# Two-layer trunk step on one core: parked latents spread over the head boundaries, two latent weights split early and parked, the last neighbourhood head and the first latent heads in another order

## The chip, the cores and the metric

The kernel runs on one core of one Trainium2 chip. The metric is device microseconds of one execution; the time before is the median of three runs, 1476.01 us (1475.26 to 1476.55). Engines are called PE (matmul), PEld (its weight loads), DVE (vector), ACT (scalar), POOL (GpSimd) and SP (which issues nearly all DMAs).

## The reference, cut to what matters

One denoising step of a two-layer backbone on 512 latent tokens and 128 prompt tokens. Layer 0 has eight latent-attention (MLA) heads and eight neighbourhood-attention heads over the same normed input; the change touches only this layer.

```python
def even_project(h, w_in, q_norm, w_uq, kv_norm, w_ukv):
    p = h @ w_in
    cq, ckv, krope, nq, nk, nv = jnp.split(p, [i0, i1, i2, i2 + na_w, i2 + 2 * na_w], axis=-1)
    q = (rms_norm(cq, q_norm) @ w_uq).reshape(b, L, MLA_HEADS, MLA_QK_DIM)
    ckv = rms_norm(ckv, kv_norm)
...
    a_mla = attend_blocked(q, jnp.concatenate([k_lat, k_ctx], axis=1),
                           jnp.concatenate([v_lat, v_ctx], axis=1), MLA_SCALE)
    a_na = neighbourhood_attention(nq, nk, nv, c_nk, c_nv, rpb)
    return jnp.concatenate([a_mla.reshape(b, L, -1), a_na.reshape(b, L, -1)], axis=-1) @ w_out
```

Neighbourhood attention lets a token see a window of 8 by 16 grid neighbours, with a bias, and 128 cached prompt tokens, in one softmax. The latent heads get their keys and values by multiplying the compressed latents `ckv` with `w_ukv`, and their queries by multiplying `cq` with `w_uq`.

## The kernel before, in words

All products are done in high and low parts: a float32 operand is copied to a reduced-precision "high" part by ACT and the rest, "low", is formed by a subtraction on DVE (for some on POOL). A product is then three matmuls, or two where one side needs no low part. A name that ends in h or l is such a part. `unit` (line 168) loads a weight into a raw buffer and splits it this way; there are three raw buffers (`rawp`, line 72) and three for split weights (`wp`).

The queue of each engine is put in order by a scheduler at build time, which may draw an instruction ahead of others that are written before it. `tc.issue_after` (through the helper `after`, line 177) bounds that: of what is issued inside it, those instructions that run on the given instruction's own engine get their places behind it, those of other engines are not held. The order of PE's work is written by hand in strings of piece names, which `sequence` (line 121) runs, each piece's matmuls behind the last matmul ahead of it. A piece issues its matmuls and the ACT, DVE and POOL work that takes their result out of PSUM.

The neighbourhood heads go one after another (line 945). Of head h, `s0` and `s1` are the score matmuls (tiles `ns`) and their softmax (`np`); `t0` to `t2` transpose the probabilities of the head before (`nt`) and split them (`nts`), `v0` to `v2` multiply them with the values (`no`), after which `half_sum` (line 411) copies half of the result (`nhs`, ACT) and adds (DVE into `oN`). `q` pieces are projections of later heads' queries and keys (`nq`, `nk`), `m` pieces are parts of a modulation product (`mod`, fed by loads `mraw`), `pt` and `pv` are transposes and values for the prompt tokens of a head pair (`npp0t`, `npp0o` and so on).

During this the latents `ckv`, `cq` and the rotary key `kr` leave the SBUF: `park` (line 845) splits each 128x640 piece (ACT `pt...h`, DVE `pt...l`) and SP stores the halves in DRAM (`pk...`). The temporaries are three buffers of one ring (`tmp`, line 103), so a fourth temporary waits until an earlier store has landed. `PARK_AT` (line 861) gives the head ahead of which each is parked; it is issued behind `PE.last`, the last matmul at that time, which holds none of it, since nothing of it runs on PE; the scheduler has put nearly all of it ahead of head 0's scores.

The last head (h = 7, the last string of `NA_ORDER`) has the first latent pieces among its own: `k0` and `k1` (`mk`) are keys of the first head pair, `u0` and `u1` (`mq`) queries of head 0. `k_set` (line 889) splits the keys. `latents`, `unpark` and `k_rope` load the parked data back. `wmv` is the value weight of all latent heads, `wm0` to `wm3` (line 838) are the key and query weights of a pair of heads, and `mv_of` makes one of six value blocks (`b0` to `b5` or `mv`): two in the row of pieces after the last head (line 1001), four after it (line 1072). The table `tq` (640 KB, line 1008) is needed for the queries of latent head 1 and later.

The latent heads (line 1080) run by `MLA_ORDER`: `s0` to `s3` are scores (`ms`) of 128 queries each, with a maximum on DVE (`mn`) and an exponential on ACT (`mp`), two score banks being there; `q0`, `q1` and `k0`, `k1` are queries of the next head (`mq`, then `mqt` on DVE, `mqh` on ACT, `mql` on POOL) and keys of the next pair; `t`, `v` and `l` are transposes (`mt`, `mts`) and value products (`mo`) of the head before.

Of the kernel before, what the change touches and what calls it, by code (L numbers as in the profile page):

```python
# [18 lines left out]
P = 128  # L19
# [32 lines left out]
def body(ctx, tc, xT, vecs, crow, wm0, wm0g1, wm0g, wm1, wA, wNV, wNA, wMK, wMV, wOA, wGQ, wGK, wGV, wOC,  # L52
# [109 lines left out]

    def load(src, n, name):
        raw = rawp.tile([P, 1024], F32, tag="raw", name=name)
        nc.sync.dma_start(raw[:, :n], src)
        return raw[:, :n]

    def unit(src, n, name, lo="v", pool=None, bufs=3):

        raw = load(src, n, name + "r")  # L170
# [240 lines left out]
    def half_sum(dsts, ps, n, pool, name):  # L411

        t = pool.tile([64, 512], F32, tag="hs", bufs=1, name=name)
        S.activation(t[:, :n], ps[64:128, :n], AF.Copy)
        for dst, a, b in dsts:
            V.tensor_tensor(dst, ps[0:64, a:b], t[:, a:b], ALU.add)

# [285 lines left out]
    nqk, wnas = {}, {}  # L703
# [77 lines left out]
    def na_scores(h, bm, pts):  # L781
# [5 lines left out]
        def piece(jj):  # L787
# [6 lines left out]
            for j in (2 * jj, 2 * jj + 1):  # L794
# [3 lines left out]
                S.activation(pt, pt, AF.Exp, bias=mm[:, j:j + 1], scale=-1.0, accum_out=ll[:, j:j + 1])  # L798
# [4 lines left out]
    def na_values(h, pts, o):  # L803
# [16 lines left out]
        def av(n):  # L820
            def run():
# [7 lines left out]
                if n == 2:  # L829
                    half_sum(((o[rr, 64:NS], 0, 448), (o[rr, 0:64], 448, NS)), box["o"], NS, ab, f"nhs{h}")  # L830
# [5 lines left out]
    wmk = {}  # L836
# [19 lines left out]

    def cached_latents():
# [4 lines left out]
               3: lambda: park("cq0", cq[0], T), 4: lambda: park("cq1", cq[1], T), 5: lambda: park("kr", kr, 768)}  # L862

    def latents():
# [12 lines left out]
    def unpark(name):  # L877
        out = [ring.tile([P, T], F32R, tag="h" + c, name=f"{name}{c}") for c in "hl"]
        for t, d in zip(out, parked[name]):
            nc.sync.dma_start(f(t), d)  # L880
# [8 lines left out]
    def k_set(r, rows, parts, src, p=0):  # L889

        jobs = []
        for c in parts:
            c0, c1 = KPART[c]
            o = c0 - KPART[parts[0]][0]
            h, l = [(prompt if c == 2 else main_[:, c0:c1])[rows] for main_, prompt in k_tiles(r, p)]
            jobs.append((h, l, src[rows, o:o + c1 - c0]))
# [11 lines left out]
    def k_pieces(p, bk):  # L908

        out = {}  # L910
        for c, n in ((0, 512), (1, 256)):
            parts = ((0,), (1, 2))[c]

            def done(ps, parts=parts):
                for r in range(2):
                    k_set(r, slice(64 * r, 64 * r + 64), parts, ps, p)
# [26 lines left out]
    NA_ORDER += ["s0 t0 t1 pt s1 m0 v0 t2 sp m1 v1 pv m2 v2", "s0 t0 t1 k0 s1 v0 t2 sp k1 v1 u0 v2 u1"]  # L943
    M_AT = 1, 3, 5, 6
    for h in range(8):
# [5 lines left out]
        if h in PARK_AT:  # L951
            after(PE.last, PARK_AT[h])
# [17 lines left out]
        if h == 7:  # L970
            cqs = after(PE.last, lambda: [unpark(f"cq{u}") for u in range(2)])
# [7 lines left out]
        if h == 6:  # L979
            mla_w(0)  # L980
            lat = latents()
# [4 lines left out]
            wmv = unit(wMV, 1024, "wmv")  # L986
        if h == 7:
            for r in range(2):
                k_rope(r, (slice(64, 128), slice(0, 64))[r])
# [1151 lines left out]
```

## Time and profile before

| | |
|---|---|
| median of three runs | 1476.01 us |
| the profiled execution's own time | 1476.62 us |
| its span in the trace | 1474.5 us |
| TensorE clock granted over it | 0.996 |
| ACT, DVE, POOL busy | 783.3, 1231.4, 175.0 us |

The span is counted from the first instruction; about 2.1 us of the execution's time lie outside of it. The stretch of the neighbourhood heads is 94 to 213 us on the trace's clock, the latent heads follow up to about 320 us. In a row of the timeline the columns are start, duration, engine, line, operation, output and inputs, form, count, and in brackets the idle time of the engine ahead of it with what ended it. PE's rows overlap: one starts before the modelled end of the row ahead, so the step from start to start is the cost of a matmul.

### The profile page before, as it was taken

Reading aid. Unit: us, or ns where it says so; the run is one execution under the profiler, and the core shown is the slowest. Engines: PE = TensorE matmul, PEld = TensorE weight load, DVE = VectorE, ACT = ScalarE, POOL = GpSimd, SP = SyncE. Lnnn points to the kernel's source line nnn. Section 1 sums busy time; section 2 is a strip of 40 time slices with the busy share of each in tenths; the row PEclk is TensorE's granted clock in tenths of the full one; section 3 lists DMA queues with packets and bytes.
Section 4 is the critical chain, followed back from the end, with each engine's and each line's share of the span. In section 5 each row is a group of like instructions: output and inputs, shape, how many; then the busy total and the mean of one; then the engine's idle time right before and its main releaser. Section 6 shows DMA issues by size and latency. Waiting matters only on the chain.

```text
span 1474.5 us, 25877 instructions
## 1 busy us (share of the span) xinstructions
PE 1440.1 (98%) x9764; PEld 1390.1 (94%) x9764; DVE 1231.4 (84%) x2350; ACT 783.3 (53%) x1530; POOL 175.0 (12%) x270
## 2 busy tenths in 40 slices
PE   5999999999999999999999999999999999999997
PEld 4988888889999999999999999989999999999997
DVE  5877668877898989965997888888899898989976
ACT  5446667763755555541122666672656555555443
POOL 0037545430000000000000122220000000000000
PEclk9999999999999999999999999999999999999999
DMA  9655471026165555569764310115245555548572
GB/s 369 211 185 194 135 243 46 15 73 200 47 202 173 168 168 170 173 223 326 241 220 155 101 34 30 43 37 194 84 169 178 184 174 185 174 147 294 185 270 72
DMA packets 84884, 239.22 MB, mean 162 GB/s; under 512 B 9496, under 2 KB 15800, under 8 KB 84376
## 3 DMA queue, kind: packets, MB, share of 16 engines
q1 hardware_dynamic: 82400, 233.16, 47.2%
q10 hardware_dynamic: 1944, 3.48, 0.7%
q8 instruction: 76, 1.25, 0.4%
q0 software_dynamic: 416, 0.93, 0.2%
q14 instruction: 48, 0.39, 0.1%
HBM read 197.21 MB, written 40.33 MB: 161 GB/s over the span
## 4 chain that ended last, share of the span: by engine, by line
PE 83%; DVE 7%; ACT 4%; DMA 3%; issue 2%; DVEq 0%; ACTq 0%; POOL 0%; SPq 0%
PE fg L64 19%; PE fd L64 9%; PE fgo L64 5%; PE fo L64 5%; PE fu L64 4%; PE gq L64 3%; PE fdo L64 2%; PE gs L64 2%; PE go L64 2%; PE nk L64 1%; PE fuo L64 1%; DMA mraw<-in_wm 1%; PE gt L68 1%; PE mod L64 1%; ACT mp L1036 1%
## 5 line engine op out<-in xcount | busy, mean ns | idle before, releaser
L1708 DVE SCALAR_TENSOR_TENSOR junk<-wm,cb 128x1024 bf16<-128x1024 f32 x88 | 107.4, 1220 | 4.6 <-DMA wm<-in_wm 3.7
L64 PE MATMUL gq<-h10h,wgq 128*128 128x320 f32 x256 | 65.8, 316 | 0.0
L267 POOL TENSOR_SCALAR h10h<-h10t,gs,mods 128x320 fp32r<-128x320 f32 x4 | 3.9, 990 | 430.1 <-DVE h10t L261 427.7
L1448 ACT ACTIVATE wY<-s 128x1024 fp32r<-128x1024 f32 x38 | 40.3, 1061 | 27.4 <-PE fg L64 22.5
L1448 ACT ACTIVATE wZ<-s 128x1024 fp32r<-128x1024 f32 x38 | 40.2, 1057 | 21.1 <-PE fd L64 16.0
L1976 POOL TENSOR_TENSOR xr<-xw,fn1rs 128x320 f32<-128x320 f32 x2 | 1.7, 861 | 412.8 <-ACT fn1rs L235 412.8
L1449 DVE TENSOR_TENSOR wZ<-s,wZ 128x1024 fp32r<-128x1024 f32 x38 | 46.4, 1222 | 2.5
L1449 DVE TENSOR_TENSOR wY<-s,wY 128x1024 fp32r<-128x1024 f32 x38 | 46.3, 1220 | 0.3
L64 PEld LDWEIGHTS gq<-h10h,wgq 128*128 128x128 f32 x256 | 44.9, 189 | 0.6
L1557 DVE TENSOR_TENSOR sg<-up,sg 128x640 f32<-128x640 f32 x38 | 31.3, 823 | 15.9 <-ACT sg L1556 14.9
L1556 ACT ACTIVATE sg<-fg 128x320 f32<-128x320 f32 x38 | 16.7, 438 | 48.4 <-PE fg L64 48.4
L1578 ACT ACTIVATE p<-fd 128x320 f32<-128x320 f32 x38 | 16.6, 437 | 46.3 <-PE fd L64 46.3
L64 PE MATMUL gq<-h10l,wgq 128*128 128x320 f32 x128 | 39.4, 308 | 0.0
L1913 ACT ACTIVATE gp<-gs,gb,rq 128x640 f32<-128x640 f32 (+1 forms) x40 | 31.8, 796 | 13.2 <-DVE gb L1912 11.8
L64 PE MATMUL fg<-h01E,wW 128*128 128x320 f32 x228 | 36.6, 309 | 0.7 <-DVE g L1588 0.7
L64 PE MATMUL fg<-h01N,wZ 128*128 128x320 f32 x228 | 36.6, 309 | 0.5 <-ACT p L1576 0.5
L64 PE MATMUL fg<-h11N,wZ 128*128 128x320 f32 x228 | 36.7, 309 | 0.0
L64 PE MATMUL fg<-h01q,wX 128*128 128x320 f32 x228 | 36.7, 309 | 0.0
L64 PE MATMUL fu<-h11q,wX 128*128 128x320 f32 x228 | 36.6, 309 | 0.0
L64 PE MATMUL fd<-h01q,wZ 128*128 128x320 f32 x228 | 36.6, 309 | 0.0
L64 PE MATMUL fd<-h11q,wZ 128*128 128x320 f32 x228 | 36.6, 309 | 0.0
L64 PE MATMUL fg<-h11q,wX 128*128 128x320 f32 x228 | 36.5, 309 | 0.0
(3416 smaller groups left out, 5296.0 us busy)
## 6 DMA issues: line engine op xcount, KB each, us to landing
wm<-in_wm SPq DMA_DIRECT2D x48, 512.0 KB, 4.3
mraw<-in_wm SPq DMA_DIRECT2D x8, 1024.0 KB, 13.1
mraw<-in_wm SPq DMA_DIRECT2D x14, 512.0 KB, 4.3
wmv<-in_wm0g SPq DMA_DIRECT2D x8, 512.0 KB, 4.1
wm<-in_wm0g SPq DMA_DIRECT2D x8, 512.0 KB, 4.7
ruo<-in_wFO SPq DMA_DIRECT2D x8, 512.0 KB, 4.3
rgo<-in_wFO SPq DMA_DIRECT2D x8, 512.0 KB, 5.5
x<-in_xT SPq DMA_DIRECT2D x8, 320.0 KB, 5.6
```

What stands on the lines that cost most here:

```text
L64: cls.last = nc.tensor.matmul(*a, **k)
L68: cls.last = nc.tensor.transpose(*a, **k)
L267: G.tensor_scalar(h[:, c0:c1], t, self.gsl[:, k, 0:1], self.ml[:, self.sh + k, 0:1], ALU.mult, ALU.add)
L1036: exps[h, j] = S.activation(halves(pt), pss[:, :, :HT], AF.Exp, bias=nm, accum_out=ll[:, j:j + 1])
L1448: S.activation(h, src, AF.Copy)
L1449: V.tensor_tensor(w_, src, f(h), ALU.subtract)
L1556: last = S.activation(sg[:, 0:HT], g[:, :HT], AF.Silu, scale=-1.0)
L1557: V.tensor_tensor(sg, up, sg, ALU.mult)
L1578: S.activation(p5, b5[:, :HT], AF.Copy)
L1708: V.scalar_tensor_tensor(junk, raw, 1.0, cb[:, c, :], ALU.mult, ALU.mult, accum_out=mods[l][:, j0 + i, c:c + 1])
L1913: gexp[h, j] = S.activation(dst, src, AF.Exp, bias=nb, scale=rq[:, j:j + 1], accum_out=ll[:, j:j + 1])
L1976: G.tensor_tensor(x[k][:, c0:c1], root[1][k], nrm.rs[:, c0:c1], ALU.mult)
```

## The change

It has five parts.

1. **Parking.** `PARK_AT[h]` is issued behind the last exponential of head h-1, an ACT instruction, instead of behind `PE.last`. So its ACT copies, and what follows from them on DVE and SP, are spread over the boundaries ahead of heads 1 to 5.
2. **Third and fourth latent weights.** `park_weights` loads `wm2` ahead of head 3 and `wm3` ahead of head 5, splits them in two pieces of 128x384 (ACT `ptwm`, the same ring of three temporaries; DVE in place) and stores them. When they are needed they come as four loads, and ACT and POOL split nothing there. `wm1` is still split, but behind `half_sum` of head 7.
3. **Last neighbourhood head.** `s1` goes directly behind `s0`; the split of `wmv` goes behind the last exponential of head 7; the parked latents are loaded behind `wm0`'s load, `cq` behind `wmv`'s, the rotary keys behind `cq`'s. `b0` and `b1` go ahead of `pt`. `k_set` does the high parts of all four tiles ahead of the low parts.
4. **First latent heads.** Heads 0 and 1 have an order of their own.
5. **A value block.** Block 5 is made between `s2` and `s3` of latent head 0.

```diff
     def mla_w(p):
         if p not in wmk:
-            wmk[p] = unit(wMK[p], 768, f"wm{p}", lo="g")
+            if f"wm{p}" in parked:
+                t = wp.tile([P, 2, 1024], F32R, tag="w", bufs=3, name=f"wm{p}")
+                for c, d in enumerate(parked[f"wm{p}"]):
+                    nc.sync.dma_start(f(t[:, c, :768]), d)
+                wmk[p] = [t[:, c, :768] for c in range(2)]
+                return wmk[p]
+            wmk[p] = after(done_with[7] if p == 1 else None, lambda: unit(wMK[p], 768, f"wm{p}", lo="g"))
         return wmk[p]
...
+    def park_weights(p):
+
+        raw = load(wMK[p], 768, f"wmp{p}r")
+        parked[f"wm{p}"] = [drc.tile([P, 768], F32, name=f"pkwm{p}{c}") for c in "hl"]
+        dh, dl = parked[f"wm{p}"]
+        for a, b in ((0, 384), (384, 768)):
+            h = tmp(f"ptwm{p}{a}")[:, :b - a]
+            S.activation(h.bitcast(F32R), raw[:, a:b], AF.Copy)
+            V.tensor_tensor(raw[:, a:b].bitcast(F32R), raw[:, a:b], h, ALU.subtract)
+            nc.sync.dma_start(dh[:, a:b], h)
+        nc.sync.dma_start(dl, raw)
...
-               3: lambda: park("cq0", cq[0], T), 4: lambda: park("cq1", cq[1], T), 5: lambda: park("kr", kr, 768)}
+               3: lambda: (park("cq0", cq[0], T), park_weights(2)), 4: lambda: park("cq1", cq[1], T),
+               5: lambda: (park("kr", kr, 768), park_weights(3))}
...
-    NA_ORDER += ["s0 t0 t1 pt s1 m0 v0 t2 sp m1 v1 pv m2 v2", "s0 t0 t1 k0 s1 v0 t2 sp k1 v1 u0 v2 u1"]
+    NA_ORDER += ["s0 t0 t1 pt s1 m0 v0 t2 sp m1 v1 pv m2 v2", "s0 s1 t0 t1 k0 v0 t2 sp k1 v1 u0 v2 u1"]
...
         if h in PARK_AT:
-            after(PE.last, PARK_AT[h])
+            after(nexps[h - 1, 3], PARK_AT[h])
...
-            cqs = after(PE.last, lambda: [unpark(f"cq{u}") for u in range(2)])
+            cqs = after(fetched["wmvr"], lambda: [unpark(f"cq{u}") for u in range(2)])
...
-            lat = latents()
+            lat = latents(fetched["wm0r"])
...
-            wmv = unit(wMV, 1024, "wmv")
+            wmvr = load(wMV, 1024, "wmvr")
         if h == 7:
-            for r in range(2):
-                k_rope(r, (slice(64, 128), slice(0, 64))[r])
+            wmv = after(nexps[7, 3], lambda: unit(None, 1024, "wmv", raw=wmvr))
+            with tc.issue_after(fetched["cq1"].ins):
+                for r in range(2):
+                    k_rope(r, (slice(64, 128), slice(0, 64))[r])
...
-    BESIDE = ()
+    BESIDE = (5,)
...
+    FIRST_ORDER = "s0 q0 s1 q1 s2 b5 s3", "k0 s0 q0 s1 t0 t1 q1 s2 v0 k1 l0 t2 s3 v1 t3 l1 v2 l2 t4"
...
-        sequence(MLA_ORDER[r], {**pieces, **late, **{k: v for k, v in tail.items() if k not in ("v3", "v4", "l3", "l4")}})
+        sequence(FIRST_ORDER[h] if h < 2 else MLA_ORDER[r], {**pieces, **late, **{k: v for k, v in tail.items() if k not in ("v3", "v4", "l3", "l4")}})
```

What stands in the queues at three places, before and now. A row gives the line, the operation, output and inputs, and the size.

First, ACT ahead of head 0, before: `ptckv10h`, `ptcq00h` and `ptcq10h` are parked latents, `nqh` and `nk` the high parts of head 0's and 1's queries and keys, `wnk` the next weight.

```order
L852 ACTIVATE ptckv10h<-ckvr_753 128x640
L724 ACTIVATE nqh_1021<-nq_1032 64x256
L724 ACTIVATE nqh_1022<-nq_1032 64x256
L724 ACTIVATE nqh_1021<-nq_1065 64x192
L173 ACTIVATE wnk_1191<-wnk1r 128x1024
L724 ACTIVATE nqh_1022<-nq_1065 64x192
L852 ACTIVATE ptcq00h<-cqr_594 128x640
L724 ACTIVATE nqh_1021<-nq_1065 64x128
L753 ACTIVATE nk_1030<-nk_1102 64x256
L852 ACTIVATE ptcq10h<-cqr_599 128x640
L724 ACTIVATE nqh_1022<-nq_1065 64x128
L753 ACTIVATE nk_1031<-nk_1102 64x256
```

The same place now:

```order
L727 ACTIVATE nqh_1021<-nq_1032 64x256
L727 ACTIVATE nqh_1022<-nq_1032 64x256
L727 ACTIVATE nqh_1021<-nq_1065 64x192
L175 ACTIVATE wnk_1191<-wnk1r 128x1024
L727 ACTIVATE nqh_1022<-nq_1065 64x192
L727 ACTIVATE nqh_1021<-nq_1065 64x128
L756 ACTIVATE nk_1030<-nk_1102 64x256
L727 ACTIVATE nqh_1022<-nq_1065 64x128
L756 ACTIVATE nk_1031<-nk_1102 64x256
```

The three parked pieces are gone from here, and their low parts from DVE likewise.

Second, ACT between the end of head 2 and head 3, before: `nhs` is the half sum of head 1's values, `npp0pth` the split of the transposed prompt probabilities of the first pair, for which PE waits.

```order
L724 ACTIVATE nqh_1562<-nq_1584 64x64
L724 ACTIVATE nqh_1563<-nq_1584 64x64
L724 ACTIVATE nqh_1562<-nq_1584 64x256
L724 ACTIVATE nqh_1563<-nq_1584 64x256
L414 ACTIVATE nhs_1698<-no_1639 64x512
L443 ACTIVATE npp1p,npp1l_1656<-npp1s_1651,npp1m_1654 128x128
L401 ACTIVATE npp0pth<-npp0t 128x256
```

Now:

```order
L861 ACTIVATE ptcq00h<-cqr_594 128x640
L727 ACTIVATE nqh_1562<-nq_1584 64x64
L873 ACTIVATE ptwm_1754<-wmp2r 128x384
L727 ACTIVATE nqh_1563<-nq_1584 64x64
L727 ACTIVATE nqh_1562<-nq_1584 64x256
L727 ACTIVATE nqh_1563<-nq_1584 64x256
L416 ACTIVATE nhs_1698<-no_1639 64x512
L873 ACTIVATE ptwm_1758<-wmp2r 128x384
L446 ACTIVATE npp1p,npp1l_1656<-npp1s_1651,npp1m_1654 128x128
L403 ACTIVATE npp0pth<-npp0t 128x256
```

A parked latent and the two pieces of `wm2` now stand here. The second piece (`ptwm_1758`) takes the buffer of `ptcq00h` and so waits until its store `pkcq0h` has landed; `npp0pth` stands behind it.

Third, SP after the last neighbourhood head, before: `wm1r` to `wm3r` and `oaw0r` are weight loads, `tq` is the query table, `kToh` a rotary key.

```order
L165 DMA wm1r<-in_wMK 128x768
L165 DMA wm2r<-in_wMK 128x768
L165 DMA wm3r<-in_wMK 128x768
L165 DMA oaw0r<-in_wOA 128x1024
L1008 DMA tq<-in_tabM 128x1280
L905 DMA kToh<-pkkrh 64x640
```

Now:

```order
L167 DMA wm1r<-in_wMK 128x768
L167 DMA oaw0r<-in_wOA 128x1024
L167 DMA oaw1r<-in_wOA 128x1024
L167 DMA oaw2r<-in_wOA 128x1024
L1037 DMA tq<-in_tabM 128x1280
L933 DMA kToh<-pkkrh 64x640
```

`tq` now stands behind `oaw2r`, which takes `wm1r`'s raw buffer and so waits until POOL has formed `wm1`'s low part. Before, `oaw0r` had that place.

More of the change, by code (lines that the diff above doesn't have):

```diff
@@ L887, in k_tiles, with k_set @@
         return odd_keys[p % 2] if r else even_keys
-    def k_set(r, rows, parts, src, p=0):
+    def k_set(parts, src, p):
         jobs = []
[L892 to L896, printed above, removed]
+        for r in range(2):
+            rows = slice(64 * r, 64 * r + 64)
+            for c in parts:
+                c0, c1 = KPART[c]
+                o = c0 - KPART[parts[0]][0]
+                h, l = [(prompt if c == 2 else main_[:, c0:c1])[rows] for main_, prompt in k_tiles(r, p)]
+                jobs.append((h, l, src[rows, o:o + c1 - c0]))
         for h, l, part in jobs:
```

31 lines of the change are left out of this document (18 added, 13 removed).

## The prediction

> **What bounds the kernel now.** I read the page's busy shares first.
>
> ```profile
> PE 1440.1 (98%) x9764; PEld 1390.1 (94%) x9764; DVE 1231.4 (84%) x2350; ACT 783.3 (53%) x1530; POOL 175.0 (12%) x270
> ```
>
> PE is the bound: no edit here takes matmuls away, so time can come only out of the 2% in which PE stands still. The table by windows says how much of that lies between 94 and 320 us, where all edited work is:
>
> ```profile
> sum 226.00, PE 217.30 PEld 194.84 DVE 176.47 ACT 161.20 POOL 117.04; mean PE 16.72 PEld 14.99 DVE 13.57 ACT 12.40 POOL 9.00
> ```
>
> 226.00 - 217.30 = 8.7 us. Short gaps under the modelled ends come on top, which I count below from start to start; still, a gain above some 10 us is out. PE's list of waits has no large one in it, but ten short ones, each at a place of its own; I looked each up in the timeline, and the edits one by one beside it. A measurement here tells 0.2%, 2.95 us, from no change, so most terms are below what it sees.
>
> **Parking, head 0.** PE's scores of head 0, the ACT row that opens the jam, and the DVE rows that close it:
>
> ```profile
> 106.68 0.74 ACT L852 ACTIVATE ptckv10h<-ckvr 128x640 fp32r<-128x640 f32 x1 [3.93 <-DMA out_o_nv<-nvf]
> 114.15 1.08 DVE L853 TENSOR_TENSOR ptcq10l<-cqr,ptcq10h 128x640 fp32r<-128x640 f32 x1
> 115.27 0.55 DVE L754 TENSOR_TENSOR nk<-nk,nk 64x384 fp32r<-64x384 f32 x1
> 113.39 0.41 PE L64 MATMUL ns<-nk,nqh 128*128 128x384 f32 x1
> 113.81 0.44 PE L64 MATMUL ns<-nk,nql 128*128 128x384 f32 x1
> 115.87 0.44 PE L64 MATMUL ns<-nk,nqh 128*128 128x384 f32 x1 [1.62 <-DVE nk L754]
> 117.38 0.34 PE L64 MATMUL ns<-nk,nql 128*128 128x384 f32 x1
> 117.81 0.41 PE L64 MATMUL ns<-nk,nqh 128*128 128x384 f32 x1
> ```
>
> ACT waits 3.93 us for a ring buffer with the query copies behind it, and a parked low part of 1.08 us stands right ahead of the `nk` part for which PE waits. In the order now both are gone. A 128x384 matmul that waits for nothing takes a step of 0.18. The steps here are 0.42, 2.06 and 0.43 (113.39 to 113.81 to 115.87; 117.38 to 117.81), so 0.24 + 1.88 + 0.25 = 2.4 over; about 0.3 more lies in the two steps at 113.05 and 115.87. What is late next is PE's own work, since `nk`'s copies then follow their matmuls at once: I take **2.7** off, 1.6 (the listed wait alone) at least. ACT and DVE do the parked work at the boundaries instead, where the trace has them idle for part of the time.
>
> **Modulation load.** Ahead of the last head PE waits for a load that has shared the queue with the unparked `cq`:
>
> ```profile
> 196.14 0.64 PE L64 MATMUL mod<-mraw,scol 128*32 128x256 f32 x8 [0.29 <-DMA mraw<-in_wm]
> ```
>
> Those loads now go behind `wm0` and `wmv`: **0.3** off, 0 to 0.4.
>
> **The new waits at the boundaries.** Before, at the boundary ahead of head 3 the ACT row `nhs`, the DVE row and PE's row follow closely; the second pair is ahead of head 5:
>
> ```profile
> 148.00 0.60 ACT L414 ACTIVATE nhs<-no 64x512 f32<-64x512 f32 x1
> 149.70 0.42 DVE L405 TENSOR_TENSOR npp0ptl<-npp0t,npp0pth 128x256 fp32r<-128x256 f32 x1
> 150.18 0.33 PE L64 MATMUL npp0o<-npp0ptl,nv 128*128 128x128 f32 x1 [0.32 <-DVE npp0ptl L405]
> 175.47 0.59 ACT L414 ACTIVATE nhs<-no 64x512 f32<-64x512 f32 x1
> 177.61 0.33 PE L64 MATMUL npp1o<-npp1ptl,nv 128*128 128x128 f32 x1
> ```
>
> PE already waits 0.32 here, so there is no slack in this chain. Now `ptwm`'s second piece stands between `nhs` and `npp0pth` and cannot start until the store `pkcq0h` has landed. The copy itself (128x384, some 0.4) would add about 0.1; the landing decides. The table of DMA issues (KB each, us from issue to landing) has these stores:
>
> ```profile
> tq<-in_tabM SPq DMA_DIRECT2D x1, 640.0 KB, 6.3
> pkckv0h<-ptckv00h SPq DMA_DIRECT2D x1, 320.0 KB, 6.0
> pkcq0h<-ptcq00h SPq DMA_DIRECT2D x1, 320.0 KB, 2.5
> pkcq0l<-ptcq00l SPq DMA_DIRECT2D x1, 320.0 KB, 4.5
> pkkrh<-ptkr0h SPq DMA_DIRECT2D x1, 320.0 KB, 2.5
> pkkrh<-ptkr640h SPq DMA_DIRECT2D x1, 64.0 KB, 3.7
> ```
>
> By the order, `pkcq0h` goes out behind a modulation load of 512 KB that itself waits for `wnq`'s split on DVE, at about 146.1 on the clock of before. Landed in 2.5 it would be in by 148.6, when `nhs` ends: cost 0.1. In 4.5, at 150.6, the chain is 2.0 late; in 6.0, 3.5 late. A store right behind a 512 KB load is nearest to `pkcq0l`'s row, 4.5: **2.0** lost. Ahead of head 5 the like piece waits for `pkkrh`, issued at about 173.65 behind a bias load of 240 KB; `nhs` ends at 176.06. Landed in 2.5 it costs 0.25, in 6.0 3.75; between the two `pkkrh` rows, at 3.1, **0.9** lost. Behind the waiting ACT instruction stand `npp0p`'s exponential, the next query copies and head 3's exponentials; the DVE low parts wait for those, and PE for `npp0ptl` first. The modulation load and `wnk3`'s load stand on SP behind the low half's store; I put their landing about 1 us ahead of need and cost them at nothing; with that cover gone the next keys are late by up to 1.5.
>
> [...]
>
> **Last head to the second latent head.** PE's rows with waits, and what else is needed:
>
> ```profile
> 205.55 0.50 PE L64 MATMUL no<-nts_0l,nv 128*128 128x512 f32 x1 [0.35 <-DVE nts_0l L405]
> 207.21 0.39 PE L64 MATMUL mk<-ckph,wm 128*128 128x256 f32 x1 [0.56 <-DVE nm L796]
> 210.95 1.47 PE L68 MATMUL nt<-ident,np 128*128 128x128 f32 x12
> 213.30 0.41 PE L68 MATMUL npp3t<-ident,npp3p 128*128 128x128 f32 x2 [0.88 <-DVE oN L416]
> 227.12 0.56 PE L64 MATMUL ms<-kTh,mqh 128*128 128x320 f32 x2 [0.49 <-ACT mp L1036]
> 231.23 0.56 PE L64 MATMUL ms<-kTh,mqh 128*128 128x320 f32 x2 [0.88 <-ACT mp L1036]
> 238.53 0.50 PE L64 MATMUL mo<-mts_0h,mv 128*128 128x512 f32 x1 [0.31 <-DVE mts_0l L405]
> 202.65 1.22 DVE L174 TENSOR_TENSOR wmv<-wmvr,wmv 128x1024 fp32r<-128x1024 f32 x1
> 226.00 0.48 DVE L928 TENSOR_TENSOR mqt<-mq,tq 128x320 f32<-128x320 f32 x1
> 218.12 0.59 ACT L414 ACTIVATE nhs<-no 64x512 f32<-64x512 f32 x1 [0.99 <-PE no L64]
> 211.62 1.82 POOL L174 TENSOR_TENSOR wm<-wm1r,wm 128x768 fp32r<-128x768 f32 x1 [0.68 <-PE nt L68]
> 213.88 0.38 SPq L1008 DMA_DIRECT2D tq<-in_tabM  x1
> 229.31 0.46 PE L64 MATMUL ms<-kTh,mqh 128*128 128x320 f32 x2
> 226.67 0.82 DVE L1032 TENSOR_REDUCE mn<-ms 128x1 f32<-128x640 f32 x1 [0.18 <-PE ms L64]
> 227.53 0.80 ACT L1036 ACTIVATE mp<-ms,mn 128x640 f32<-128x640 f32 x1
> 210.69 0.84 ACT L173 ACTIVATE wm<-wm1r 128x768 fp32r<-128x768 f32 x1
> ```
>
> The bracketed waits add up to 3.5. From start to start, above the steps of like rows that don't wait, they hold 0.5, 0.7, 1.1 (behind the transposes), 0.65, 1.0 and, with the step behind 238.53, 0.8: 4.8 in all. The new orders put work into each: `s1` beside `s0` brings the softmax forward, `b0` and `b1` stand where `npp3t` waited for a bank, block 5 (no new work, it stood ahead of `s0`) stands between the third and fourth scores, `k0` where head 1's first scores waited for `mp`. Three things are late next.
>
> *`wmv`'s low part.* It was formed at 202.65 to 203.87. Now it stands behind `oN` and the last query product, which I lay at 211.2, so it ends at 212.4. PE, earlier by 0.5 + 0.7, is through its transposes at 210.9 and needs it in `b0`'s second matmul at about 211.0: **1.4** lost.
>
> *The table `tq`.* It went out at 213.88. Now it is behind `oaw2r`, that behind `wm1`'s low part on POOL (1.82), that behind `wm1`'s copy on ACT, that behind `nhs`, which with PE's lead ends near 217.5: copy to 218.2, POOL to 220.05, `tq` out at 220.5 and, by its row of 6.3, in at 226.8. On DVE the product `mqt` that needs it stands ahead of the maximum of the second scores: 226.8 + 0.45 for it + 0.8 for the maximum + 0.85 for the exponential is 228.9, when the fourth scores get their bank (the second's). Without it PE would be there at 227.7: 229.31 before, less 0.9 of lead (0.5 + 0.7 + 1.1 - 1.4) and the 0.65. **1.2** lost.
>
> *Head 1.* DVE's low parts of the first keys still stand ahead of the products PE waits for; of the 0.8 I let 0.65 stay.
>
> 4.8 - 1.4 - 1.2 - 0.65 = **1.5** off; 3.4 if `tq` is early and head 1 is smooth, 0.3 if only the 3.5 of the brackets can be won. The splits of `wm2` and `wm3` that leave ACT and POOL stood in waits for `mp` that are counted here already; the four loads that replace them are needed only by heads 3 and 5, tens of us later, and cost nothing. `k_set`'s order shifts which low part PE waits for in later heads and comes to nothing.
>
> **Sum.** 2.7 + 0.3 - 2.0 - 0.9 + 1.5 = 1.6 us off the profiled execution's 1476.62: 1475.0. That execution is 0.6 above the median of the runs, so against the median the forecast is 1476.0 - 1.6 = **1474.4 us**.
>
> **The rivals.**
>
> *Stores and table in time (0.27).* If both stores land in 2.5 as in their own rows, the boundary terms are 0.35 instead of 2.9: 4.2 off, 1471.8. If `tq` is early as well, 1.9 more: 6.1 off, 1469.9. For it: the two stores' own rows, and the few transfers of this window (the column ahead of the last is the DMA engines' share):
>
> ```profile
> 145.00:155.00 10.00, 9.68 (x80) 8.54 (x79) 7.57 (x26) 7.19 (x23) 6.20 (x13) 1.00 0.27 76
> ```
>
> Against it: the window was light because no such store and no load of `wm2` lay in it.
>
> *ACT held at both boundaries (0.13), the side of slower.* It stands behind two stores, and every softmax behind it. The gains are 2.7 + 0.3 + 1.5 = 4.5; from a landing of 4.6 us in both stores they are used up (2.1 + 2.35); at 6.0, as for `pkckv0h`, 3.5 + 3.75 - 4.5 = 2.75 lost, 1478.8; with the load of `wnk3` pushed past its need, 1.5 more. For it: the same kind of store in the busy stretch at 101 us. Against it: the queue here is less full.
>
> *The jam only moves (0.15).* The parked copies at heads 1 and 2 push back exponentials as they pushed back `nk`; ACT and DVE have to do the same 0.74 and 0.8 to 1.1 us per piece. The 2.7 falls to its lower end and the 1.5 to 0.3, and the sum is 1.6 + 0.3 + 0.3 - 2.9 = 0.7 lost: 1476.7. Against it: at the boundaries ACT has idle times of 0.3 to 2 us.
>
> **How the numbers follow.** The forecast has 0.45, with 1473.0 to 1475.6 as its own range. Faster by over 0.2% (below 1473.06) needs most of the first rival, 0.27, and the upper edge of the forecast, 0.08: 0.35. Slower by over 0.2% (above 1478.96) is the worse half of the second rival: 0.07. The rest, 0.58, is no change. The range leaves out the part of the first rival in which everything is early (0.1) and the worse part of the second (0.1): 1470.5 to 1477.8.
>
> **What would show it.** Right: no `ns` wait for `nk` at head 0; `ptwm` idle for a DMA of 2 us on ACT at about 150 and of 0.5 to 1 at 177, with `npp0o` and `npp1o` late behind it; `mv` waiting 1.4 for `wmv`; `mqt` waiting for `tq`, and `ms` late with it. Wrong: stores landing well under 4 us, `tq` issued before 217, or an exponential of heads 1 to 4 behind a parked copy with PE idle after it.

## The result, and the profile after

| | before | after |
|---|---|---|
| median (lowest to highest), six runs each | 1475.70 us (1475.26 to 1480.39) | 1484.21 us (1482.02 to 1488.41) |
| ratio of the times, 95% interval | | 1.0054 (1.0035 to 1.0073) |
| profiled execution's own time, and its span | 1476.62, 1474.5 us | 1484.23, 1482.3 us |
| TensorE clock granted over the span | 0.996 | 0.995 |

The changed kernel is some 8 us slower. The forecast was 1474.4, in a range of 1470.5 to 1477.8: the sign was wrong, and the time lies outside of the range.

The page's busy shares after the change, and the table by windows for the same 226 us as before:

```profile
PE 1442.8 (97%) x9764; PEld 1391.0 (94%) x9764; DVE 1231.4 (83%) x2354; ACT 782.6 (53%) x1532; POOL 171.9 (12%) x268
```

```profile
94.00:320.00 226.00, 213.14 (x1453) 191.29 (x1451) 170.19 (x426) 154.94 (x379) 110.18 (x181) 0.98 0.42 134
```

PE has the same 9764 matmuls, and now stands still for 12.9 of these 226 us, where it was 8.7. The column behind the busy times is the granted clock, and here it is 0.98. Such a column was 1.00 in the same stretch before. That is the first sign of a cost that the prediction did not have.

For the rest one view does most of the work. I take each PE row's start, subtract the start of the same row in the trace of before, and take the median of these shifts over 10 us of the kernel before. Where the shift grows, time is lost. All columns are profiled executions (e4 to e9 are experiments, below):

| at (us) | place | after | e4 | e5 | e6 | e7 | e8 | e9 |
|---|---|---|---|---|---|---|---|---|
| 100 | start of head 0 | -1.73 | -0.72 | -1.36 | -1.97 | -1.58 | -0.73 | -0.73 |
| 130 | head 1 | -4.30 | -3.25 | -3.93 | -4.54 | -1.76 | 0.29 | -3.27 |
| 160 | behind the boundary ahead of head 3 | 0.89 | 0.77 | -3.20 | 0.69 | -1.48 | 1.19 | -2.56 |
| 180 | behind the boundary ahead of head 5 | 3.67 | 1.65 | -2.31 | 1.04 | -1.48 | 1.19 | -1.68 |
| 240 | end of latent head 1 | 2.70 | -0.55 | -4.11 | 1.08 | -0.14 | 0.81 | -4.84 |
| 320 | end of the latent heads | 6.18 | -0.56 | -4.16 | 1.05 | 0.21 | 4.01 | -4.86 |
| 1440 | end | 7.47 | 0.00 | -4.21 | 1.14 | 0.22 | 4.40 | -2.33 |

The first row is no gain of the change: it differs between kernels that are alike there, as does the time at half clock in the first 30 us (6.83 us before, 3.41 after). All costs are counted from it, so the change loses 6.18 + 1.73 = 7.9 us up to 320.

Three places hold that loss. The first is the boundary ahead of head 3, with PE's row and the ACT rows ahead of it:

```profile
149.06 0.33 PE L64 MATMUL npp0o<-npp0pth,nv 128*128 128x128 f32 x1 [3.16 <-ACT npp0pth L403]
139.90 1.06 ACT L175 ACTIVATE wnq<-wnq3r 128x1024 fp32r<-128x1024 f32 x1 [1.85 <-DMA wnq3r<-in_wNA]
146.09 0.59 ACT L416 ACTIVATE nhs<-no 64x512 f32<-64x512 f32 x1
147.73 0.52 ACT L873 ACTIVATE ptwm<-wmp2r 128x384 fp32r<-128x384 f32 x1 [1.04 <-DMA pkcq0h<-ptcq00h]
143.29 0.33 SPq L864 DMA_DIRECT2D pkcq0h<-ptcq00h  x1
```

The wait for the store is there as drawn. But ACT has also waited 1.85 for the load of `wnq3` some 8 us earlier. The same row before:

```profile
139.10 1.06 ACT L173 ACTIVATE wnq<-wnq3r 128x1024 fp32r<-128x1024 f32 x1 [0.71 <-DMA wnq3r<-in_wNA]
```

The second place is the boundary ahead of head 5, where PE waits and ACT does not:

```profile
179.27 0.33 PE L64 MATMUL npp1o<-npp1pth,nv 128*128 128x128 f32 x1 [1.24 <-ACT npp1pth L403]
176.89 0.38 ACT L727 ACTIVATE nqh<-nq 64x256 fp32r<-64x256 f32 x1 [0.87 <-DVE nql L728]
177.29 0.59 ACT L416 ACTIVATE nhs<-no 64x512 f32<-64x512 f32 x1
177.94 0.52 ACT L873 ACTIVATE ptwm<-wmp3r 128x384 fp32r<-128x384 f32 x1
```

`ptwm` starts 0.06 behind the end of `nhs` and shows no idle time: the store had landed by then.

Behind both boundaries lies something else, in the windows ahead of, within and behind them (PE busy stands behind the length, the granted clock third from the end):

```profile
147.00:150.42 3.42, 1.23 (x7) 1.09 (x8) 2.10 (x7) 2.04 (x7) 0.38 (x1) 1.00 0.57 216
150.42:153.83 3.41, 3.41 (x18) 3.41 (x16) 2.32 (x10) 1.99 (x7) 2.57 (x5) 0.50 0.26 78
177.72:181.13 3.41, 2.04 (x14) 1.64 (x13) 2.76 (x9) 2.61 (x9) 0.38 (x1) 1.00 0.77 284
181.13:184.55 3.42, 3.42 (x19) 3.42 (x18) 2.69 (x11) 2.50 (x7) 3.02 (x5) 0.50 0.54 155
```

For 3.41 us PE runs at half its clock (0.50), once behind each of the two waits. PE counts as fully busy there, so no list of waits shows it. Each costs 1.55 in the shifts.

The third place is the later latent heads. PE's rows with the longest waits there:

```profile
239.29 0.38 PE L64 MATMUL mq<-cq0h,wm 128*128 128x320 f32 x1 [0.85 <-DVE kTol L928]
267.06 0.47 PE L64 MATMUL mo<-mts_0h,mv 128*128 128x512 f32 x1 [0.78 <-DVE kTl L928]
293.10 0.47 PE L64 MATMUL mo<-mts_0h,mv 128*128 128x512 f32 x1 [1.22 <-DVE kTol L928]
312.51 0.56 PE L64 MATMUL ms<-kToh,mqh 128*128 128x320 f32 x2 [1.27 <-ACT mp L1065]
```

The shift goes from 2.70 to 6.18 between 240 and 320 us, where the prediction had nothing. Not all of these waits are new. Before, the first two rows do not wait at all, but the third already waits 1.05 and the fourth 0.92. From row to row the shift grows by 1.09 at the first, of which 0.85 comes back within the next 2.1 us, by 0.81 at the second, by 0.17 at the third and by 0.38 at the fourth. The rest comes in steps of 0.2 to 0.5, two of them at scores (`ms`) that wait for `mp`. PE's row and DVE's order at the second of these places, before:

```profile
262.78 0.50 PE L64 MATMUL mo<-mts_0h,mv 128*128 128x512 f32 x1
261.44 0.68 DVE L900 TENSOR_TENSOR kTl<-mk,kTh 64x512 fp32r<-64x512 f32 x1 [0.25 <-ACT kTh L898]
262.05 0.67 DVE L405 TENSOR_TENSOR mts_0l<-mt,mts_0h 128x512 fp32r<-128x512 f32 x1
262.65 0.67 DVE L405 TENSOR_TENSOR mts_1l<-mt,mts_1h 128x512 fp32r<-128x512 f32 x1
263.36 0.69 DVE L900 TENSOR_TENSOR kTl<-mk,kTh 64x512 fp32r<-64x512 f32 x1
```

ACT's two high parts and DVE's order after:

```profile
264.31 1.18 ACT L926 ACTIVATE kTh<-mk 64x512 fp32r<-64x512 f32 x2
265.52 1.39 DVE L928 TENSOR_TENSOR kTl<-mk,kTh 64x512 fp32r<-64x512 f32 x2 [0.85 <-ACT kTh L926]
266.95 0.69 DVE L407 TENSOR_TENSOR mts_0l<-mt,mts_0h 128x512 fp32r<-128x512 f32 x1
267.55 0.68 DVE L407 TENSOR_TENSOR mts_1l<-mt,mts_1h 128x512 fp32r<-128x512 f32 x1
```

Before, the first low part starts when ACT has made one high part, and the second stands behind the two `mts` rows. Now ACT makes both high parts first. DVE stands idle for 0.85 until they are there, then forms both low parts, and PE's `mo`, which had no wait, waits 0.78 for the second.

### The profile page after: what moved, and what is told of

Its sections match the earlier page's. It is cut to its first block, busy times and chain, and to the rows that moved or that the text cites. A ratio compares the mean times of both kernels' runs of the same rounds, so it can differ in the third digit from the quotient of the medians.

```text
span 1482.3 us, 25896 instructions
## 1 busy us (share of the span) xinstructions
PE 1442.8 (97%) x9764; PEld 1391.0 (94%) x9764; DVE 1231.4 (83%) x2354; ACT 782.6 (53%) x1532; POOL 171.9 (12%) x268
## 3 DMA queue, kind: packets, MB, share of 16 engines
q10 hardware_dynamic: 1944, 3.48, 0.7%
## 4 chain that ended last, share of the span: by engine, by line
PE 78%; DVE 10%; DMA 6%; ACT 3%; issue 2%; DVEq 0%; ACTq 0%; POOL 0%; SPq 0%
PE fg L64 16%; PE fd L64 7%; PE fgo L64 5%; PE fo L64 5%; PE fu L64 4%; PE gq L64 3%; PE fdo L64 2%; PE nk L64 2%; PE gs L64 2%; PE go L64 2%; PE fuo L64 1%; PE gt L68 1%; PE mod L64 1%; PE nq L64 1%; DVE junk L1738 1%
## 5 line engine op out<-in xcount | busy, mean ns | idle before, releaser
L64 PE MATMUL fg<-h01C,wY 128*128 128x320 f32 x228 | 36.8, 310 | 0.8 <-ACT u L1612 0.6
```

The source lines that it names most:

```text
L64: cls.last = nc.tensor.matmul(*a, **k)
```

## The experiments

My theory after the result: the loss is (a) the new order inside `k_set`, (b) ACT's waits at the two boundaries, and (c) the half clock that these set off; the gain at head 0 is real. The rival is the prediction's own account, in which the stores alone decide and `k_set` comes to nothing. The first four kernels ran together, against 1476.15 us for the kernel before in 22 runs.

**e1: the changed kernel without the parked weights.**

```diff
-               3: lambda: (park("cq0", cq[0], T), park_weights(2)), 4: ...
-               5: lambda: (park("kr", kr, 768), park_weights(3))}
+               3: lambda: park("cq0", cq[0], T), 4: ...
+               5: lambda: park("kr", kr, 768)}
```

> The changed kernel without the parked weights: the third and fourth latent weights are split where they are needed, as before; all else as changed. Theory: the two ACT copies that stand behind a store are gone, so PE's waits of 3.2 and 1.2 us for the split prompt probabilities go, and with them the two stretches of half clock that follow (1.55 us each): about 7.3 us less than the changed kernel's 1484.2, so 1477, less what the two splits cost among the latent heads (up to 1 us). Rival: the half clock isn't caused by those idle times; then only 4.4 us go and the clock still falls to 0.5 somewhere between 140 and 190 us: 1480.

Measured 1483.18 (1481.48 to 1484.83), ratio 1.0047 (1.0030 to 1.0063): a miss. The store waits are gone, and two others have come:

```profile
139.39 1.06 ACT L175 ACTIVATE wnq<-wnq3r 128x1024 fp32r<-128x1024 f32 x1 [5.39 <-DMA wnq3r<-in_wNA]
```

```profile
141.12 0.50 PE L64 MATMUL no<-nts_0h,nv 128*128 128x512 f32 x1 [2.88 <-ACT nts_0h L403]
237.04 0.33 PE L68 MATMUL mt<-ident,mp 128*128 128x128 f32 x1 [1.54 <-POOL mp L395]
```

ACT waits 5.39 for the load of `wnq3`, and its copies for the values (`nts`) stand behind that. The load landed at 139.4, much as in the changed kernel (139.9), where two of these copies stand ahead of the wait. Though PE waits 2.88 here, and 1.87 for `npp0pth` behind it, this execution has no half clock between 140 and 190 us. And POOL, which splits `wm2` and `wm3` itself here, is late with head 1's probabilities. So the loads on SP are a cost of their own, and the parked weights are a gain of their own at 237 us.

**e2: the second `ptwm` piece in a ring of its own**, so that it waits for no store (pieces of 448 and 320 columns; the ring `u` holds tiles up to half the width):

```diff
-        for a, b in ((0, 384), (384, 768)):
-            h = tmp(f"ptwm{p}{a}")[:, :b - a]
+        for a, b in ((0, 448), (448, 768)):
+            h = (tmp(f"ptwm{p}{a}") if a == 0 else tp.tile([P, HT], F32, tag="u", bufs=7, name=f"ptwm{p}{a}"))[:, :b - a]
```

> The changed kernel with the second piece of each parked weight in another ring of temporaries (448 and 320 columns in place of 384 and 384), so that it waits for no store; everything else as changed, the parked weights too. Theory: as with the parked weights left out, 7.3 us less: 1477. It tells the store's wait from the split work itself: if the work and not the wait holds ACT, PE still waits at least 2 us at the boundary ahead of head 3 and the time stays above 1480.

Measured 1480.26 (1477.80 to 1481.85), ratio 1.0025 (1.0016 to 1.0035): a miss by 3 us. The loss ahead of head 3 falls from 3.65 to 1.78, ahead of head 5 from 1.23 to 0.89, and this execution has no half clock there. Both pieces now stand ahead of `nhs` on ACT, so the second brings neither its wait for the store (1.04) nor its copy (0.52) between `nhs` and `npp0pth`; the wait for `wnq3` also happens to be 1.28 instead of 1.85. So the second piece accounts for about half of the first term at most and for little of the second. The later latent heads still lose 3.2.

**e3: the old order inside `k_set`** (e4 has the same edit):

```diff
-        for h, l, part in jobs:
-            S.activation(h, part, AF.Copy)
-        for h, l, part in jobs:
-            V.tensor_tensor(l, part, f(h), ALU.subtract)
+        for half in (jobs[:len(parts)], jobs[len(parts):]):
+            for h, l, part in half:
+                S.activation(h, part, AF.Copy)
+            for h, l, part in half:
+                V.tensor_tensor(l, part, f(h), ALU.subtract)
```

> The changed kernel with the key splits in the order of before (high and low parts of one half of the rows, then of the other). Theory: the 3.5 us that PE loses between 246 and 326 us, with waits for kTl and kTol that before does not have, come from this order alone: 1484.2 - 3.5 = 1480.7, and the waits of mo for kTl and kTol are gone. Rival: they come from the new order of the first latent heads or from the weights' loads; then nothing changes, 1484.

Measured 1480.47 (1478.86 to 1482.12), ratio 1.0030 (1.0019 to 1.0041), as expected. The shift is 3.52 at 240 and 3.52 at 320: the later latent heads lose nothing. What is left is the boundaries, with three stretches at half clock in this execution (from 145.4, 152.2 and 182.9).

**e4: e2 and e3 together.**

> Both: the second weight piece in another ring, and the key splits in the order of before. Theory: the parts add, 1484.2 - 7.3 - 3.5 = 1473.4, faster than the kernel before by 2 to 3 us, which is what the parking at head 0 had won. Rival: something else late fills the room, and it comes out at 1476 or above.

Measured 1477.24 (1474.77 to 1479.15), ratio 1.0009 (0.9999 to 1.0018): the theory's 1473.4 missed, and the rival's 1476 or above came out. What still holds it back stands at one place, ACT's row and PE's:

```profile
142.65 1.06 ACT L175 ACTIVATE wnq<-wnq3r 128x1024 fp32r<-128x1024 f32 x1 [3.56 <-DMA wnq3r<-in_wNA]
```

```profile
145.44 0.51 PE L64 MATMUL no<-nts_2h,nv 128*128 128x256 f32 x2 [1.62 <-ACT nts_2h L403]
```

The load takes 7.4 us to land here, against 3.8 before: SP now sends `pkckv1h` and `pkckv1l` (320 KB each) and `wmp2r` (384 KB) right ahead of it. A stretch at half clock follows the wait, from 146.15.

The next four ran together, against 1476.31 us in 31 runs.

**e5: e4 with that load sent first.** Its tile is loaded behind `wnk2`, `ckv1`'s stores and `wmp2r` go behind it, and ACT's copy keeps its place:

```diff
...
+        if h == 2:
+            ahead[3, 0] = load(wNA[3, 0], 1024, "wnq3r")
+            after(nexps[1, 3], PARK_AT[2])
...
-                nc.sync.dma_start(d[:, a:b], t)
+                after(fetched["wnq3r"] if name == "ckv1" else None, lambda: nc.sync.dma_start(d[:, a:b], t))
```

> The changed kernel with the old order inside k_set, the second ptwm piece in a ring of its own (both as in the run before), and with the load of wnq3 ahead of the stores pkckv1h, pkckv1l and of the load of wmp2r on SP; ACT's copy of wnq3 keeps its place. Theory (what is left of the loss is ACT waiting for wnq3's load, which stood behind 1024 KB of new transfers and landed in 7.4 us, and the half clock that this wait sets off): the load goes out some 2 us earlier and lands in about 4, ACT waits under 0.5 for it, no<-nts_2h on PE waits under 0.4 instead of 1.62, and no half clock follows near 146. PE's rows at 157 stand about 3.2 earlier than in the run before, so the median is 1473 to 1474.5, 2 to 3 below the kernel before. Rival (the load's lateness is only moved: ckv1's stores and what follows them land later, and cost the same at head 3): npp0pth or wmp2r's copy waits 1.5 or more in its place, 1476.5 to 1477.5.

Measured 1473.07 (1471.98 to 1476.05), ratio 0.9981 (0.9972 to 0.9989): as expected, and faster than before. ACT's row has no wait, and PE's largest at the boundary is 0.84:

```profile
138.50 1.06 ACT L175 ACTIVATE wnq<-wnq3r 128x1024 fp32r<-128x1024 f32 x1
146.44 0.33 PE L64 MATMUL npp0o<-npp0pth,nv 128*128 128x128 f32 x1 [0.84 <-ACT npp0pth L403]
```

The boundary ahead of head 3 now costs 0.73 (-3.93 to -3.20), without half clock. The load left at 132.64 instead of 135.21 and landed in 5.8: still late, but in time.

**e6: the kernel before with the spread parking alone.**

```diff
-            after(PE.last, PARK_AT[h])
+            after(nexps[h - 1, 3], PARK_AT[h])
```

> The kernel before with the spread parking alone: no wm2 or wm3 parked, all other orders as before. By the prediction's terms, which put no price on the parking at the boundaries where no weights are split: -2.7, so 1473.4 or so with before at 1476. Theory (the parked stores of ckv1 go ahead of wnq3's load, and the ACT copy of wnq3 stands ahead of nts_0h as in the kernel before): -2.6 at head 0, but the load lands in 5.5 to 6.5 instead of 3.8, ACT waits 2.5 to 5 for it, PE 2 to 4 at no<-nts_0h and, where half a clock window is idle, a half-clock stretch of 1.5 on top: between -0.5 and +3, so 1475.5 to 1479. npp0pth waits little (no ptwm ahead of it): under 1.

Measured 1479.59 (1477.18 to 1481.72), ratio 1.0021 (1.0010 to 1.0032). Head 0 gains 2.57 (-1.97 to -4.54), and the boundary ahead of head 3 takes 5.2 back:

```profile
139.11 1.06 ACT L173 ACTIVATE wnq<-wnq3r 128x1024 fp32r<-128x1024 f32 x1 [5.26 <-DMA wnq3r<-in_wNA]
140.84 0.50 PE L64 MATMUL no<-nts_0h,nv 128*128 128x512 f32 x1 [2.75 <-ACT nts_0h L401]
150.37 0.33 PE L64 MATMUL npp0o<-npp0pth,nv 128*128 128x128 f32 x1 [1.86 <-ACT npp0pth L401]
```

There is no `ptwm` here, and yet `npp0o` waits 1.86, where I had said under 1. The late `wnq` is not the whole of that. From the first of the `nqh` copies to `nhs` ACT takes 3.24 here and took 2.28 before, and what stands between them now is the parked `cq0`, its copy on ACT (0.72) and its low part on DVE:

```profile
146.59 0.83 DVE L853 TENSOR_TENSOR ptcq00l<-cqr,ptcq00h 128x640 fp32r<-128x640 f32 x1 [0.39 <-ACT ptcq00h L852]
```

So about 1.0 of this wait goes with the parked piece itself. The rest came out as the theory had it.

**e7: the new last head and first latent heads alone** (e1 and e3's edits, and the parking at `PE.last`).

> The changed kernel with the old parking, without wm2 and wm3 parked and with the old order in k_set: what is left is the last neighbourhood head, its loads, the first latent heads' orders and block 5. By the prediction's terms (0.3 for the modulation load, 1.5 from the last head to the second latent head, the wm2 and wm3 splits counted in waits that are gone anyway): -1.8, 1474.2. Theory: -0.5 for the modulation load stays, but with wm2 and wm3 split on POOL again behind wm1, which now starts later, the mp of head 1 wait on POOL for 1 to 1.5 as in the run without parked weights, and a half-clock stretch can follow: -0.5 to +2, so 1475.5 to 1478. Heads 2 to 8 of the latent part shift by 0.

Measured 1477.28 (1475.95 to 1479.62), ratio 1.0008 (0.9999 to 1.0016). Up to 225 us this part gains 2.2 (-1.58 to -3.78), and then one row gives it back:

```profile
234.19 0.33 PE L68 MATMUL mt<-ident,mp 128*128 128x128 f32 x1 [1.54 <-POOL mp L395]
```

A second wait of 0.45 for POOL and a half-clock stretch from 235.4 follow. So these orders are worth nothing without the parked `wm2` and `wm3`, which take their splits off POOL.

**e8: the kernel before with the new order inside `k_set` alone.**

> The kernel before with the new order inside k_set alone: four high parts on ACT, then four low parts on DVE, instead of two and two. By the prediction (comes to nothing): 1476.0, within 0.3. Theory (the third and fourth ACT copies push exponentials and query copies back, the low parts come in a block of four on DVE, and PE waits for kTl and kTol): heads 1 to 7 lose 0.8 to 1.3 at each new pair of keys, three pairs, +3.3 in all: 1479.3, all of it between 246 and 326 us.

Measured 1479.61 (1477.20 to 1481.75), ratio 1.0022 (1.0013 to 1.0030). The 1.0 lost in the table between 100 and 130 us is not the edit's: PE waits 1.62 for `nk` at 115.21, as before, and a half-clock stretch follows here. The first keys, near 207 us, gain 1.2, and the later pairs lose 4.4 from 230 us on, 1.2 of it ahead of the stretch that I named:

```profile
239.00 0.47 PE L64 MATMUL mo<-mts_0h,mv 128*128 128x512 f32 x1 [1.13 <-DVE kTol L902]
290.94 0.47 PE L64 MATMUL mo<-mts_0h,mv 128*128 128x512 f32 x1 [1.25 <-DVE kTol L902]
```

The last three ran together, against 1476.93 us in 15 runs.

**e9: e5 with the load of `oaw2r` held behind that of `tq`.**

```diff
-    x, pend = mixer_out(wOA, ... True)
+    x, pend = mixer_out(wOA, ... True, hold=fetched["tq"])
```

> The run with wnq3's load first, with the load of oaw2r held behind the load of tq on SP; nothing else changed. Theory (the table tq is late because it stands behind oaw2r, which waits for wm1's split on POOL): tq goes out at about 211 instead of 218.31 on that run's clock, mqt does not wait for it, and the second scores' mp is in time: the ms wait of 0.63 and most of the 0.51 and of the steps around them go, 0.7 to 1.5 less, 1471.6 to 1472.4. By the prediction's term for tq: 1.2 less. Rival (the fourth scores wait for the softmax chain of DVE and ACT in any case): 0.3 or less, 1473.

Measured 1472.35 (1471.32 to 1474.39), ratio 0.9973 (0.9964 to 0.9982): the lowest median of all, 4 us below the kernel before. By the two ratios the step from e5 is 1.2 us, but their intervals overlap. `tq` leaves at 211.80 instead of 218.31, no `ms` of the first two latent heads waits over 0.4 for `mp`, and the stretch from 180 to 240 gains 3.16 where e5 gains 1.80: 1.36 for the table.

**e10 and e11: the clock by itself.** Both are the kernel before with ten more ACT copies in all that rewrite the same values: e10 all at `npp0pth`, e11 three, three, two and two at `npp0pth` to `npp3pth`.

```diff
-        S.activation(shape(h), ps, AF.Copy)
+        for _ in range(1 + {'npp0pt': 10}.get(name, 0)):
+            S.activation(shape(h), ps, AF.Copy)
```

> The kernel before with the ACT copy npp0pth (128x256) made eleven times instead of once; the ten more rewrite the same values and are there to delay PE at npp0o ahead of head 3 in one lump. Theory (a window of 3.41 us in which PE is busy for less than half is followed by one at half the clock): ten copies at a step of about 0.3 are 3.0 to 3.5 us of standstill at npp0o, which fills over half of at least one window wherever the windows lie; a stretch of 3.41 us at half clock follows within 3.4 us and costs 1.5 to 1.7 more: 4.5 to 5.2 later than before in the profile from 160 us on, 1480.5 to 1481.5 by the clock of the runs. Rival (the stretches at half clock come by themselves): 3.0 to 3.5 later, 1479 to 1479.8, with no more half clock than the kernel before has.

> The same ten extra copies, but three at npp0pth, three at npp1pth, two at npp2pth and two at npp3pth. Theory: each standstill is 0.6 to 1.3 us and stays under half a window, so no half clock is set off that the kernel before does not have; the four delays add up to 2 to 3.3 at most (less where PE had slack): 1478 to 1479.3, 1.5 to 3 below the lump. Rival (the lateness of ACT alone makes the price, whatever its distribution): the same as the lump within 0.5.

e10 measured 1482.63 (1482.01 to 1483.84), ratio 1.0045 (1.0033 to 1.0058). e11 measured 1481.61 (1480.21 to 1484.19), ratio 1.0041 (1.0026 to 1.0056). The standstills were longer than I had put them, since other ACT rows stand among the copies: 4.99 in e10, 1.37 and 1.31 in e11. The windows of e10 around its one:

```profile
149.60:153.00 3.40, 0.17 (x2) 0.00 (x0) 1.43 (x6) 3.23 (x11) 0.72 (x2) 1.00 0.07 21
153.00:156.40 3.40, 1.64 (x6) 1.47 (x7) 0.72 (x2) 1.83 (x6) 2.51 (x4) 0.50 0.00 0
156.40:159.80 3.40, 3.40 (x16) 3.40 (x15) 1.94 (x8) 1.57 (x6) 1.77 (x4) 0.50 0.00 0
159.80:163.20 3.40, 3.40 (x35) 2.68 (x34) 1.29 (x2) 1.06 (x2) 0.25 (x1) 1.00 0.13 33
```

The window in which PE is busy for 0.17 us is followed by one at half clock (0.50); in that one PE is busy for 1.64 of 3.40, and another at half clock follows. The shift grows by 6.9, of which 4.7 is the wait itself (4.99 less the 0.32 of before), so I put 2.2 down to the clock. The windows of e11 around its two waits, on a grid of 3.41 us:

```profile
145.70:149.10 3.40, 2.58 (x19) 2.31 (x18) 1.91 (x6) 2.84 (x9) 1.45 (x3) 1.00 0.30 83
149.10:152.50 3.40, 2.72 (x19) 2.58 (x20) 2.58 (x9) 2.42 (x8) 1.51 (x3) 1.00 0.00 0
176.40:179.80 3.40, 1.96 (x12) 1.55 (x11) 1.95 (x7) 2.75 (x10) 0.53 (x2) 1.00 0.00 0
179.80:183.20 3.40, 3.40 (x17) 3.40 (x17) 2.17 (x10) 1.81 (x6) 3.16 (x6) 0.50 0.02 5
```

The first wait, 1.37 long, ends at 149.65: the border at 149.10 cuts it, the two windows are busy for 2.58 and 2.72 us, and the clock stays at 1.00. The second, 1.31 long, ends at 178.39 and lies within one window, which is busy for 1.96, 58%: half clock (0.50) follows, and the shift grows by 2.87 here, 1.56 more than the wait. My expectation that waits of up to 1.3 set off no half clock was wrong, and the runs of e11 are 1.0 below e10's, not 1.5 to 3, with intervals that overlap. What e11's execution shows is that two waits of nearly one length, 1.37 and 1.31, cost 1.2 and 2.9, and that a border of the grid cuts the first and not the second.

## Why the prediction was wrong, point by point

In the shifts up to 320 us, the prediction's terms against what they measured in the changed kernel (minus is gained):

| term | predicted | measured |
|---|---|---|
| parking, head 0 | -2.7 | -2.57 |
| waits ahead of head 3 | +2.0 | +3.65 |
| waits ahead of head 5 | +0.9 | +1.23 |
| modulation load, and last head to second latent head | -1.8 | -0.97 |
| `k_set`'s order, later latent heads | 0 | +3.48 |
| half clock, two stretches | none | +3.10 |
| sum | -1.6 | +7.92 |

*Parking, head 0: right.* 2.57 came off here in the changed kernel, and likewise in e6, where it stands alone.

*The failed step: "`k_set`'s order shifts which low part PE waits for in later heads and comes to nothing".* I gave it no row and no term. The order does more than shift which low part PE waits for. With the high parts first, DVE starts on the low parts later (0.85 idle at 265.52, where it was 0.25), both come ahead of `mts_0l`, and PE waits where it did not wait before: 0.85 at 239.29 and 0.78 at 267.06. Only at 293.10 did the remark nearly hold. PE's row there, before:

```profile
287.79 0.49 PE L64 MATMUL mo<-mts_0h,mv 128*128 128x512 f32 x1 [1.05 <-DVE mts_0l L405]
```

It waited 1.05 for `mts_0l` and now waits 1.22 for `kTol`, and the shift grows by 0.17 alone. That the order is the cause is shown from both sides: e3 and e4 take it back and lose nothing between 240 and 320; e8 has it alone and loses 4.4 from 230 on, 3.2 with what it gains at the first keys.

*The missing term: the clock.* The prediction let a wait cost its own length. Two waits of 3.16 and 1.24 cost 1.55 more each, because the windows that they end in, in which PE is busy for 1.23 and 2.04 us, are each followed by 3.41 us at half clock (0.50). I had seen the granted clock of 1.00 in this stretch of before and taken it for given.

*Waits ahead of head 3: the mechanism was right, and only part of it.* `pkcq0h` went out at 143.29, which is 147.6 on the clock of before (I had 146.1), and landed in 4.3 (I had 4.5). But the runs part the 3.65 roughly into three: up to 1.9 goes with the second piece of `ptwm` behind `nhs` (3.65 to 1.78 in e2), about 1.0 with `wnq3`'s late load (1.78 in e2 to 0.73 in e5), and 0.7 stays for the copies and low parts that are left, for which the prediction had 0.1. Each of these is from one execution, and they scatter: e4, alike with e2 here, waits 3.56 for `wnq3` instead of 1.28 and loses 4.0, some 2.4 of it apart from its half clock.

*The step that missed `wnq3`.* Of the loads pushed back on SP, the prediction named the modulation load and `wnk3`'s. The load that mattered is `wnq3`'s, behind two stores and a load of 1024 KB together. Before, ACT already waited 0.71 for it, a row that I had not looked for. In e6 the row that waits for it takes 3.5, more than the 2.57 that the parking gains.

*Waits ahead of head 5: near the right size, by luck.* The price was put on the landing of `pkkrh`. It landed in 3.4, at 177.86, just as `nhs` ended, so ACT did not wait. With a ring of its own, 0.89 of the 1.23 remains, so most of it is the added work on ACT and DVE. In e6, where `kr` alone is parked here, the boundary takes 0.35 (0.69 to 1.04), so some 0.5 goes with the pieces of `wm3`; whether ACT or DVE decides was not parted.

*Last head to the second latent head: right size, spoiled by `k_set`.* With the old `k_set`, the stretch from 180 to 240 gains 2.2 in e3 and e4, against 1.8 predicted; in the changed kernel 1.2 of that is missing by 240, with the wait of 0.85 for `kTol` at 239.29. `wmv` cost 0.74, not 1.4. The table `tq` was costed at 1.2 and is worth 1.36 in e9. The remark that the splits of `wm2` and `wm3` stood in waits "counted here already" was half of it: with the new orders they would have cost 1.54 and 0.45 (e7).

*The rivals.* "ACT held at both boundaries" had the right sign and 1478.8, by landings of 6.0. The landings were 4.3 and 3.4; by that mechanism alone I estimate the change at near nothing (4.5 gained, some 3 and 1 lost). No rival had the clock or `k_set`.

Two things stay open. Behind 320 us, which the change does not touch, executions differ by up to 2.5: in the table e9 goes from -4.86 to -2.33. 1.57 of that is a half-clock stretch from 862.50 to 865.91, and e1 has the like from 873.93; the rest was not traced. And why the stores of 320 KB land in 3.3 to 4.7 us at the boundaries of the changed kernel, and not in 2.5, was not shown.

## What to carry to other kernels

An edit that only reorders rows on one engine needs its own line in the sum: find the row that PE waits for, and see whether the new order puts anything ahead of it or starts it later. When stores move to a place where a load is already waited for, list every load behind them on the queue, and look for each one's waiting row before, even where it is only 0.7 us. And a wait on PE can cost more than its length: here waits of 1.24, 1.31 and 3.16 us each brought 1.55 or 1.56 us more by the clock, and one of 1.37 brought none, so such a wait is to be priced with that chance.

## What the runs showed of the hardware

The half clock comes in stretches of 3.41 us (6.83 in e10, and in the first 30 us of before). In the changed kernel's trace the stretches lie on one grid: one ends at 24.13, and the next two begin at 150.42 and 181.13, which is 126.29 and then another 30.71 us further on, 37.0 and 9.0 times the 3.413 that a stretch lasts there. In other executions the grid lies elsewhere: in e10 and e11 stretches begin at 153.00 and 179.80, 0.8 and 8.6 such steps behind 150.42. I cut eleven traces into windows along their grids between 96 and 318 us. All 13 windows that half clock follows have PE busy for at most 60% by the profile's modelled ends. Four of them are at 46% or less, and no window that low was without half clock behind it; between 47 and 60% nine windows were followed by it and nine were not. These traces show no sharper border than that, and the same wait falls on either side of it: behind the 1.62 of before, which ends at 115.87, the clock stayed at 1.00, and in e8, where it ends at 115.21, half clock began at 115.04. The price is not always 1.55: in head 0, in e8 and e10, the shift grew by only 1.0 over such a stretch.

Outside of the edited part a stretch came behind a fuller window. The window ahead of e9's late stretch, and the stretch:

```profile
859.08:862.50 3.42, 2.90 (x21) 2.37 (x21) 3.39 (x8) 1.70 (x5) 0.60 (x1) 1.00 0.20 53
862.50:865.91 3.41, 3.41 (x15) 3.41 (x16) 2.52 (x6) 2.39 (x6) 0.00 (x0) 0.50 0.26 103
```

PE counts as busy for 2.90 of 3.42 us there, 85%. Ten of its matmuls have only two columns each (`gr`, 128x2); without them it is 2.0 us, 59%. Why half clock follows this window was not shown.

Of the changed kernel's two waits at the boundaries, the shorter, of 1.24 us, ends at 179.27 in a window in which PE stands still for 1.37 of 3.41 us in all, and half clock follows.

The granted clock also differs between the runs. The changed kernel's two fastest runs, 1482.02 and 1482.32, have a granted clock of 0.996 and 0.997, and the slowest, 1488.41, has 0.993. A stretch of 3.41 us at 0.50 is worth 1.7 of 1482 us by estimate, 0.001 of the mean clock.
